# GLA state of 128 columns, output norms' Newton steps on GpSimd, and three smaller moves in a decoder trunk

## The chip, the cores and the metric

The kernel runs on one core of a Trainium2 chip, as one program and one launch. The metric is the device time in microseconds. Before the change the median of three runs is 2576.46 us (2575.63 to 2578.42). A core has TensorE (PE, with its weight loads shown as PEld), VectorE (DVE), ScalarE (ACT) and GpSimd (POOL); transfers are issued by SP, a few by POOL.

## The reference

One layer of a decoder trunk on x of 2048 x 1024 in float32, conditioned by a vector c:

- mod = silu(c) @ w_ada + b_ada gives six vectors of 1024: shift, scale and gate for each of two sub-layers.
- Token mixer: h = rmsnorm(x) (1 + sc1) + sh1; one input projection; then three groups of causal heads. Four retention heads (rotary q and k, fixed decay per head), eight HGRN2 heads (forget f = lb + (1 - lb) sigmoid(z), key (1 - f), 64 key channels), four GLA heads (decay exp(logsigmoid(...)/16), 32 key channels). All values have 64 columns per head. HGRN2 and GLA are the same recurrence with a decay per key channel:

```
S_t = diag(f_t) S_{t-1} + k_t^T v_t,   o_t = q_t S_t
```

- Each head's output is RMS-normed and multiplied by silu of a gate; the heads are joined, scaled by head_gain, and go through w_out; x += g1 * result.
- Channel mixer: norm and modulation again, up-projection to 2 x 2816, causal depthwise convolution of width 3, silu(gate) * value, down-projection; x += g2 * result. A final RMS norm with gain.

## The kernel before, in words

The sequence goes in four blocks of 512 positions (b = 0 to 3), each of four chunks of 128. Activations lie transposed (channels on the 128 partitions, positions along the columns). Every large product is made of three matmuls of a high and a low part (`split3`, L246 to L248). The token mixers take the first 1250 us; then the up and down products follow for two halves of the sequence.

A block runs the units h0, g, h1, h2, h3, r0, r1: two HGRN2 heads (h), all four GLA heads (g), two retention heads (r). A unit first makes its projections and query, key and decay tiles, then gives a chain of small steps (`gated`, `retention`) to a clock. The clock holds the order of TensorE, which is fixed by the program: it counts estimated microseconds of matmul time, and when a due time has passed, the next step of a chain is issued between the large matmuls. A step that comes too early on TensorE waits for the other engines. `LEVEL_GAP`, `POST_GAP` (12.0) and the `gap` of `rstd` are such due times. VectorE, ScalarE, GpSimd and SP are ordered by the planner of the framework, by priority and its own estimates (`tc.high_priority` moves instructions ahead); each runs its list in order.

`gated` works through seven levels (1, 2, 4 ... 64 positions): per level a matmul of keys with queries (L622), an update of the queries and keys by the decays (L630, L632), and a copy into the attention tile (L638, L641). Then the keys are transposed, the state gets its four updates (L671), `attn_out` adds attention times values and queries times state (L575 to L581), and `post` norms the output per head: square (L546), sum (L548), a reciprocal square root by a magic number and three Newton steps (`newton`, L153 to L158, each step three VectorE instructions), scaling (L552) and gate (L553). `transposed` (L559 to L562) brings it to channels on partitions, as high and low parts, for the output projection in two halves of four key tiles (`out_half`; the second half of block b comes after the first unit of block b + 1).

Query tiles `q` (128 x 2 x 512, a ring of three) hold head 0 in slot 0 and head 1 in slot 1, with zeros in the other head's rows, so that one matmul serves both heads. For HGRN2 both heads are merged into one tile `qn` before `attn_out` (L655), and the state has 128 columns, one block of 64 per head. For GLA the state has 64 columns, and each head has a matmul of its own with it (L581). GLA is done in two halves of two heads.

`ada` makes one of the 48 columns of mod: a load of 512 KB, a sum on VectorE (L197). The list `later` gives one to each weight piece that follows. Weights' low parts, and for w_out the high parts too, are made in block 0 and kept in HBM. `rstd` is the norm of a whole row: sums by a matmul (L325), Newton on VectorE, and after `gap` a broadcast by matmul (L335). `weight_sums` prepares sums of the channel mixer's weights. `vec` holds all per-channel vectors (245 columns).

Of the kernel before, what the change touches and what calls it, by code (L numbers as in the profile page):

```python
# [100 lines left out]
def trunk(ctx, tc, xT, vecs, cvec, cst, rope, msk, wada, win, walow, wgla, wout, wup, wdown, out):  # L101
# [38 lines left out]
    vec = pc.tile([P, NV], F32, tag="vec", name="vec")  # L140
    nc.sync.dma_start(vec[:], vecs)
    c_all = pc.tile([P, NC_], F32, tag="cst", name="c_all")
    m_all = p1.tile([P, 448], U32, tag="msk", name="m_all")
# [7 lines left out]
    def newton(x, y, n):  # L151

        V.tensor_scalar(y[:].bitcast(I32), x[:].bitcast(I32), -0.5, MAGIC, op0=ALU.mult, op1=ALU.add)  # L153
        a = small("nw", n)
        for _ in range(3):
            V.scalar_tensor_tensor(a[:], y[:], -0.5, y[:], op0=ALU.mult, op1=ALU.mult)
            V.tensor_tensor(a[:], a[:], x[:], op=ALU.mult)
            V.scalar_tensor_tensor(y[:], a[:], 1.5, y[:], op0=ALU.add, op1=ALU.mult)  # L158
# [53 lines left out]
    def piece(src, name, key, gain=None, ahead=50):  # L212

        if later:
            ada(later.pop(0))
        with tc.high_priority(offset=ahead):
            hi = pw.tile([P, 1024], F32R, tag="whi", name="h" + name)
            lo = pw.tile([P, 1024], F32R, tag="wlo", name="l" + name)
            if key + "h" in kept:
                nc.sync.dma_start(hi[:].bitcast(F32), kept[key + "h"][:])  # L220
                nc.sync.dma_start(lo[:].bitcast(F32), kept[key + "l"][:])
                return hi, lo
            raw = pw.tile([P, 1024], F32, tag="wraw", name="r" + name, bufs=NRAW)
            nc.sync.dma_start(raw[:], src)
            if gain is None:
                S.copy(hi[:], raw[:])
                if key + "l" in kept:
                    nc.sync.dma_start(lo[:].bitcast(F32), kept[key + "l"][:])
                else:
                    V.tensor_tensor(lo[:], raw[:], hi[:], op=ALU.subtract)  # L230
                    keep(key + "l", lo[:])
            else:
                n = 1024 // len(gain)
                for i, g in enumerate(gain):
                    sl = slice(i * n, (i + 1) * n)
                    S.activation(hi[:, sl], raw[:, sl], AF.Copy, scale=g)
                for i, g in enumerate(gain):
                    sl = slice(i * n, (i + 1) * n)
                    V.scalar_tensor_tensor(lo[:, sl], raw[:, sl], g, hi[:, sl], op0=ALU.mult, op1=ALU.subtract)
                keep(key + "h", hi[:])  # L240
                keep(key + "l", lo[:])
        return hi, lo
# [271 lines left out]
    states = [p1.tile([P, NS, 64 if i == 4 else P], F32, tag=f"S{i}", name=f"S{i}") for i in range(7)]  # L514
    for i, st in enumerate(states):
        if i != 4:
            G.memset(st[:], 0.0)
# [24 lines left out]
    def post(o, sg, name):  # L542
# [5 lines left out]
        V.tensor_reduce(ms[:], sq[:].rearrange("p (a e) -> p a e", e=64), axis=mybir.AxisListType.X, op=ALU.add)  # L548
        V.tensor_scalar(ms[:], ms[:], 1.0 / 64, EPS, op0=ALU.mult, op1=ALU.add)
        rs = small("ors" + name)  # L550
        newton(ms, rs, 8)
        V.tensor_tensor(o8, o8, rs[:].unsqueeze(2).to_broadcast([P, 8, 64]), op=ALU.mult)  # L552
        V.tensor_tensor(o[:], o[:], sg[:], op=ALU.mult)  # L553

    def transposed(b, pos, o, name):

        ps = late_ps("oT" + name)
        for c in range(NCH):
            T.transpose(ps[:, c * P:(c + 1) * P], o[:, c, :], ident)  # L559
        oT = pa.tile([P, 2, TB], F32R, tag="a4k", name="oT" + name)  # L560
        S.copy(oT[:, 0, :], ps[:])
        V.tensor_tensor(oT[:, 1, :], ps[:], oT[:, 0, :], op=ALU.subtract)  # L562
        oTs[b][pos] = oT

    def attn_out(name, b, attn, v, q, Sst, qn=None):

        ps = late_ps("o" + name)
        for c in range(NCH):
            oc = ps[:, c * P:(c + 1) * P]
            cs = slice(c * P, (c + 1) * P)  # L570
            inter = not (b == 0 and c == 0)
            both = inter and qn is not None
            st = Sst[:, (b * NCH + c) % NS, :]
            if both:
                T.matmul(oc, qn[:, cs], st, start=True, stop=False)  # L575
            for hh in range(2):
                oo = oc[:, hh * 64:hh * 64 + 64]
                T.matmul(oo, attn[:, (c * 2 + hh) * P:(c * 2 + hh + 1) * P], v[:, c, hh * 64:hh * 64 + 64],
                         start=not both, stop=hh == 1 if both else not inter)
                if inter and not both:  # L580
                    T.matmul(oo, q[:, hh, cs], st, start=False, stop=True)  # L581
        return ps
# [15 lines left out]
    def gated(name, b, ui, pos, kq, decay, subs, qk, sel):  # L598
# [45 lines left out]
        qn = None  # L644
# [4 lines left out]
        with tc.high_priority(offset=CHAIN):  # L649
            S.copy(kT[:].rearrange("p c n -> p (c n)"), ps[:])  # L650
            if not two:
                q, rows = subs[0][:2]
                qn = late("qn" + name)
                for hh, (r0, r1) in enumerate(rows):
                        S.copy(qn[r0:r1, :], q[r0:r1, hh, :])  # L655
        adv(4 * MF)
        yield 1.8
        for q, rows, v, sg in subs:
# [3 lines left out]
            with tc.high_priority(offset=CHAIN):  # L662
                for c in range(NCH):
                    for hh, (r0, r1) in enumerate(rows):
                        es = slice(0, 64) if two else slice(64 * hh, 64 * hh + 64)
# [10 lines left out]
        for i, ((q, rows, v, sg), at) in enumerate(zip(subs, attns)):  # L676
# [8 lines left out]
            ps = attn_out(f"{name}_{i}", b, at, v, q, Sst, qn)  # L685
# [13 lines left out]
    def unit_h(b, u, pos):  # L699
# [17 lines left out]
        q = new_qbd(nm, rows)  # L717
        for hh, (r0, r1) in enumerate(rows):
            V.tensor_tensor(q[r0:r1, hh, :], sq[r0:r1, :], f[r0:r1, :], op=ALU.mult)
# [16 lines left out]
    def unit_g(b, pos):  # L736
# [27 lines left out]
        V.tensor_tensor(qk[:], qs[:], kq[:], op=ALU.mult)  # L764
        decay = decays(f, e)
        subs = []
        for i in range(2):
            rows = [(32 * i, 32 * i + 32), (64 + 32 * i, 96 + 32 * i)]
            q = new_qbd(f"{nm}_{i}", rows)
            for hh, (r0, r1) in enumerate(rows):  # L770
                V.tensor_tensor(q[r0:r1, hh, :], qs[r0:r1, :], f[r0:r1, :], op=ALU.mult)
# [40 lines left out]
    def retention(nm, b, r, pos, a, kk, kc, q, vsg):  # L812
# [47 lines left out]
        ps = attn_out(nm, b, at, v, q, Sst, qn)  # L860
        o = pu.tile([P, NCH, P], F32, tag="o", name="o" + nm)
        qd = c_all[:, C_QD + 2 * r:C_QD + 2 * r + 2]
        with tc.high_priority(offset=CHAIN):
# [3 lines left out]
            post(o, sg, nm)  # L867
# [34 lines left out]
    def out_half(b, half, acc=None, after_pieces=None):  # L902
        hg = [vec[:, V_HG + 4 * half + k:V_HG + 4 * half + k + 1] for k in range(4)]
        ops = [oTs[b][4 * half + k] for k in range(4)]
        for i in range(4):
            wp = piece(wout[half * 4 + i], f"wo{b}_{half}_{i}", f"o{half * 4 + i}", gain=hg, ahead=250 if (b, half) == (0, 0) else 600 if (b, half) == (NB - 1, 1) else 50)
# [19 lines left out]
    def out_finish(b, after_pieces=None):  # L926
# [16 lines left out]
        clock.at(4.0, rstd(acc, f"n2_{b}", bc[:], then if b else lambda: put_off.append(then)))  # L943
# [90 lines left out]
    nc.sync.dma_start(m_all[:], msk)  # L1034
# [4 lines left out]
    for b in range(NB):  # L1039
        pos = 0  # L1040
        if b == 1:
            later += range(24, 40)
        if b == 2:
            later += range(40, 48)
        for i, (kind, u) in enumerate(ORDER):
# [6 lines left out]
            if b == 1 and i == 2:  # L1052
# [8 lines left out]
            if b and i >= (3 if b == 1 else 1):  # L1061
                for _ in range(2 if b == 2 else 1):
# [111 lines left out]
    def conv(s, u, t, y):  # L1174
        cw = vec[:, V_CW + 3 * t:V_CW + 3 * t + 3]
        S.activation(y[:], u[:, 2:SB + 2], AF.Identity, bias=vec[:, V_CB + t:V_CB + t + 1], scale=cw[:, 2:3])
# [98 lines left out]
    def down_norm(s, h, y, acc, bc, bank=None):  # L1275
        b = 2 * s + h

        def scale(m):
            V.scalar_tensor_tensor(y[h, m], y[h, m], vec[:, V_FG + m:V_FG + m + 1], bc[:], op0=ALU.mult, op1=ALU.mult)
# [25 lines left out]
    def last_product(s, y, acc):  # L1305
# [28 lines left out]
        def norm(t, p, sq, banks):  # L1334
# [11 lines left out]
            def scale(m, bc):  # L1346
                V.scalar_tensor_tensor(y[1, m][:, cols], y[1, m][:, cols], vec[:, V_FG + m:V_FG + m + 1], bc[:, 0:n],
# [82 lines left out]
    halo = pg.tile([P, 2 * NF + 4, 2], F32, tag="halo", name="halo")  # L1430
    with tc.high_priority(offset=100):
# [122 lines left out]
```

## Time and profile before

| | |
|---|---|
| median of three runs | 2576.46 us |
| profiled execution | 2570.92 us |
| its span in the trace | 2569.2 us |
| PE busy | 2500.8 us (97%) |
| DVE busy | 1990.3 us (77%) |
| ACT busy | 1117.5 us (43%) |
| POOL busy | 157.4 us (6%) |

The profile is one execution, taken by the hardware profiler. A row of a group gives line, engine, operation, tiles (out <- in), shapes and count, then busy us, mean ns of one, and the idle time before them with what ended it. A row of waits reads: engine, line, what it waited for, us in total, times, longest. A row of the timeline gives start, duration, engine, line, operation and tiles. A row on one source line gives min/median/max ns, first and last start. The time of the execution outside the span is 1.7 us.

### The profile page before, as it was taken

What the parts mean: (1) busy time and instruction counts of PE and PEld (TensorE: products, weight loads), DVE (VectorE), ACT (ScalarE), POOL (GpSimd) and SP (SyncE); (2) the same over time, 40 slices, a digit from 0 to 9 for tenths busy, and PEclk for the clock granted to TensorE, in tenths of its full rate; (3) what the DMA queues carried; (4) which work ended last, traced back from release to release, by engine and by line L of the source; (5) the groups of instructions that cost most, each with busy time, mean ns of one, the idle gap of its engine ahead of it and who ended that gap; (6) DMA issues with size and microseconds to landing.
All of it is one profiled execution on the core that took longest, in us unless ns stands there. A gap on an engine that the chain in (4) does not pass through costs nothing.

```text
span 2569.2 us, 37237 instructions
## 1 busy us (share of the span) xinstructions
PE 2500.8 (97%) x13206; PEld 2138.0 (83%) x13206; DVE 1990.3 (77%) x3648; ACT 1117.5 (43%) x1898; POOL 157.4 (6%) x270
## 2 busy tenths in 40 slices
PE   5999999999999999999999999999999999999998
PEld 4798878998889888998778888888878888888887
DVE  8778986868778786887678888887687778778666
ACT  3333434433343234433355545555444555455442
POOL 1000010000000000000010000000011001000000
PEclk9999999999999999999999999999999999999999
DMA  8543656765687856877664444477675444447653
GB/s 304 193 161 132 215 216 231 275 218 178 213 313 262 294 175 209 314 269 257 210 241 166 162 135 164 156 255 249 216 230 172 149 153 145 147 141 247 224 192 128
DMA packets 231242, 533.89 MB, mean 208 GB/s; under 512 B 25072, under 2 KB 28176, under 8 KB 231056
## 3 DMA queue, kind: packets, MB, share of 16 engines
q1 hardware_dynamic: 229136, 525.23, 60.0%
q0 software_dynamic: 1920, 6.29, 0.6%
q8 instruction: 104, 1.70, 0.3%
q14 instruction: 82, 0.67, 0.1%
HBM read 397.72 MB, written 133.69 MB: 207 GB/s over the span
## 4 chain that ended last, share of the span: by engine, by line
PE 87%; DVE 7%; DMA 3%; ACT 1%; issue 1%; SPq 0%; DVEq 0%; ACTq 0%
PE X L246 6%; PE X L247 6%; PE X L248 6%; PE lvh L622 3%; PE Z L247 3%; PE Z L246 3%; PE Z L248 3%; PE dX L247 3%; PE dX L246 3%; PE dX L248 3%; PE psqkvgr L248 2%; PE psqkvgr L246 2%; PE psqkvgr L247 2%; PE psvgh L246 2%; PE psvgh L247 2%; PE psvgh L248 2%
## 5 line engine op out<-in xcount | busy, mean ns | idle before, releaser
L246 PE MATMUL X<-B,A 128*128 128x512 f32 x572 | 223.9, 391 | 1.4 <-ACT u L1242 1.4
L247 PE MATMUL X<-B,A 128*128 128x512 f32 x572 | 223.2, 390 | 0.3 <-DMA B<-made 0.3
L248 PE MATMUL X<-B,A 128*128 128x512 f32 x572 | 223.1, 390 | 0.0
L973 DVE TENSOR_TENSOR dA<-rd,dA 128x512 fp32r<-128x512 f32 x154 | 106.0, 689 | 89.5 <-ACT dA L972 89.1
L972 ACT CAST dA<-rd 128x512 fp32r<-128x512 f32 x154 | 95.6, 621 | 142.8 <-PE dX L248 46.7
L973 DVE TENSOR_TENSOR A<-s,A 128x512 fp32r<-128x512 f32 x176 | 120.6, 686 | 40.7 <-ACT A L972 40.7
L246 PE MATMUL psvgh<-hvgh,ha 128*128 128x256 f32 x480 | 140.4, 293 | 0.0
L246 PE MATMUL dX<-dB,dA 128*128 128x512 f32 x352 | 136.9, 389 | 0.0
L247 PE MATMUL dX<-dB,dA 128*128 128x512 f32 x352 | 136.9, 389 | 0.0
L248 PE MATMUL dX<-dB,dA 128*128 128x512 f32 x352 | 136.9, 389 | 0.0
L248 PE MATMUL psvgh<-hvgh,ha 128*128 128x256 f32 x480 | 136.0, 283 | 0.0
L247 PE MATMUL psvgh<-lvgh,ha 128*128 128x256 f32 x480 | 136.0, 283 | 0.0
L972 ACT CAST A<-s 128x512 fp32r<-128x512 f32 x176 | 108.4, 617 | 62.6 <-PE Z L248 46.8
L246 PEld LDWEIGHTS X<-B,A 128*128 128x128 f32 x572 | 107.7, 188 | 25.3 <-ACT u L1242 2.2
L247 PEld LDWEIGHTS X<-B,A 128*128 128x128 f32 x572 | 107.7, 188 | 23.1 <-DMA B<-made 1.0
L248 PEld LDWEIGHTS X<-B,A 128*128 128x128 f32 x572 | 107.7, 188 | 22.3
L246 PE MATMUL Z<-B,A 128*128 128x512 f32 x308 | 120.6, 392 | 2.5 <-ACT B L972 1.7
L622 PEld LDWEIGHTS lvh<-qbh,kh 128*128 128x128 f32 x896 | 115.8, 191 | 7.5 <-issue 1.1
L247 PE MATMUL Z<-B,A 128*128 128x512 f32 x308 | 120.7, 392 | 0.3 <-DVE B L973 0.3
L622 PE MATMUL lvh<-qbh,kh 128*128 128x128 f32 x896 | 120.7, 277 | 0.3 <-DVE kh L632 0.3
L248 PE MATMUL Z<-B,A 128*128 128x512 f32 x308 | 120.4, 391 | 0.0
L973 DVE TENSOR_TENSOR dB<-rb,dB 128x512 fp32r<-128x512 f32 x154 | 105.3, 685 | 9.5 <-ACT dB L972 9.4
(457 smaller groups left out, 7133.3 us busy)
## 6 DMA issues: line engine op xcount, KB each, us to landing
gs<-yv SPq DMA_DIRECT2D x154, 256.0 KB, 2.9
rb<-gs SPq DMA_DIRECT2D x154, 256.0 KB, 4.0
r<-wup SPq DMA_DIRECT2D x141, 256.0 KB, 3.4
s<-sumsu SPq DMA_DIRECT2D x132, 256.0 KB, 3.0
wada<-wada SPq DMA_DIRECT2D x48, 512.0 KB, 4.8
rd<-sumsd SPq DMA_DIRECT2D x88, 256.0 KB, 4.0
rd<-wdown SPq DMA_DIRECT2D x66, 256.0 KB, 3.7
x<-xT SPq DMA_DIRECT2D x64, 256.0 KB, 4.8
```

Source lines behind the costliest of these rows:

```text
L246: T.matmul(ps, lhs[0], rhs[0], start=first, stop=False, skip_group_check=more)
L247: T.matmul(ps, lhs[0], rhs[1], start=False, stop=False, skip_group_check=more)
L248: T.matmul(ps, lhs[1], rhs[0], start=False, stop=last, skip_group_check=more)
L622: T.matmul(ps[:, c * P:(c + 1) * P].rearrange("p (h n s) -> p h n s", h=2, s=s), kq[:, c * P:(c + 1) * P], rhs, start=True, stop=True)
L972: S.copy(hi, src)
L973: V.tensor_tensor(lo, src, hi, op=ALU.subtract)
```

## The change

- The state of the GLA has 128 columns, like the others. The queries of the second head are copied into slot 0 at the end of the levels, for HGRN2 and GLA (the tile `qn` of HGRN2 is gone), and `attn_out` has one form: one matmul with the state per chunk, then one with the attention per head.
- `newton` has a form on GpSimd, with four instructions a step; `post` uses it, but for the last unit of the last block.
- Queries are multiplied by the decay once for all rows on VectorE; ScalarE then copies the heads into `q`.
- head_gain is applied where the outputs are transposed, no longer to the weights.
- The conditioning sums 24 to 39 begin after the first unit of block 1. The norm of block 0's rows that needs them moves from the third to the fourth unit of block 1, and weight sums begin one unit later, with two in the last unit.
- The norms of the blocks' inputs and of the rows of blocks 0 to 2 have a gap of 8.0 instead of 4.5 between their two steps on TensorE.
- `vec` holds 117 columns; convolution weights and final gain come in a second tile, loaded before the last output half. The mask tile loads 320 of 448 columns.

```diff
     def newton(x, y, n, relaxed=False):
         V.tensor_scalar(y[:].bitcast(I32), x[:].bitcast(I32), -0.5, MAGIC, op0=ALU.mult, op1=ALU.add)
         a = small("nw", n)
         for _ in range(3):
+            if relaxed:
+                G.tensor_tensor(a[:], y[:], y[:], op=ALU.mult)
+                G.tensor_tensor(a[:], a[:], x[:], op=ALU.mult)
+                G.tensor_scalar(a[:], a[:], -0.5, 1.5, op0=ALU.mult, op1=ALU.add)
+                G.tensor_tensor(y[:], a[:], y[:], op=ALU.mult)
+                continue
             V.scalar_tensor_tensor(a[:], y[:], -0.5, y[:], op0=ALU.mult, op1=ALU.mult)
...
-        clock.at(22.0, rstd(acc, f"n1_{b}", bc1[b][:], lambda: done.add(("n1", b))))
+        clock.at(22.0, rstd(acc, f"n1_{b}", bc1[b][:], lambda: done.add(("n1", b)), gap=8.0))
...
-    states = [p1.tile([P, NS, 64 if i == 4 else P], F32, tag=f"S{i}", name=f"S{i}") for i in range(7)]
+    states = [p1.tile([P, NS, P], F32, tag=f"S{i}", name=f"S{i}") for i in range(7)]
...
-        newton(ms, rs, 8)
+        newton(ms, rs, 8, relaxed)
...
-        S.copy(oT[:, 0, :], ps[:])
-        V.tensor_tensor(oT[:, 1, :], ps[:], oT[:, 0, :], op=ALU.subtract)
+        g = vec[:, V_HG + pos:V_HG + pos + 1]
+        S.activation(oT[:, 0, :], ps[:], AF.Copy, scale=g)
+        V.scalar_tensor_tensor(oT[:, 1, :], ps[:], g, oT[:, 0, :], op0=ALU.mult, op1=ALU.subtract)
...
-    def attn_out(name, b, attn, v, q, Sst, qn=None):
+    def attn_out(name, b, attn, v, qn, Sst):
         ps = late_ps("o" + name)
         for c in range(NCH):
             oc = ps[:, c * P:(c + 1) * P]
             inter = not (b == 0 and c == 0)
-            both = inter and qn is not None
-            if both:
-                T.matmul(oc, qn[:, cs], st, start=True, stop=False)
+            if inter:
+                T.matmul(oc, qn[:, c * P:(c + 1) * P], Sst[:, (b * NCH + c) % NS, :], start=True, stop=False)
             for hh in range(2):
...
-                if inter and not both:
-                    T.matmul(oo, q[:, hh, cs], st, start=False, stop=True)
...
-            if not two:
-                q, rows = subs[0][:2]
-                qn = late("qn" + name)
-                for hh, (r0, r1) in enumerate(rows):
-                        S.copy(qn[r0:r1, :], q[r0:r1, hh, :])
+            for q, rows, v, sg in subs:
+                r0, r1 = rows[1]
+                S.copy(q[r0:r1, 0, :], q[r0:r1, 1, :])
...
+        V.tensor_tensor(sq[:], sq[:], f[:], op=ALU.mult)
         for hh, (r0, r1) in enumerate(rows):
-            V.tensor_tensor(q[r0:r1, hh, :], sq[r0:r1, :], f[r0:r1, :], op=ALU.mult)
+            S.copy(q[r0:r1, hh, :], sq[r0:r1, :])
...
-            post(o, sg, nm)
+            post(o, sg, nm, (b, r) != (NB - 1, 1))
...
-            wp = piece(wout[half * 4 + i], f"wo{b}_{half}_{i}", f"o{half * 4 + i}", gain=hg, ahead=...)
+            wp = piece(wout[half * 4 + i], f"wo{b}_{half}_{i}", f"o{half * 4 + i}", both=True, ahead=...)
...
-        clock.at(4.0, rstd(acc, f"n2_{b}", bc[:], then if b else lambda: put_off.append(then)))
+        clock.at(4.0, rstd(acc, f"n2_{b}", bc[:], then if b else lambda: put_off.append(then), gap=8.0 if b < NB - 1 else 4.5))
...
-        if b == 1:
-            later += range(24, 40)
...
+            if b == 1 and i == 0:
+                later += range(24, 40)
-            if b == 1 and i == 2:
+            if b == 1 and i == 3:
                 assert not later
                 clock.until(lambda: put_off)
                 put_off.pop()()
...
-            if b and i >= (3 if b == 1 else 1):
-                for _ in range(2 if b == 2 else 1):
+            if b and i >= (4 if b == 1 else 1):
+                for _ in range(2 if b == 2 or (b, i) == (1, 6) else 1):
                     weight_sums(*jobs.pop(0))
...
+    vec2 = pg.tile([P, NV - V_CW], F32, tag="vec2", name="vec2")
+    nc.sync.dma_start(vec2[:], vecs[:, V_CW:NV])
```

GLA's query part has the same form as HGRN2's, with two halves of 32 rows per head.

More of the change, by code (lines that the diff above doesn't have):

```diff
@@ L210, in trunk, with piece @@
     later = []
-    def piece(src, name, key, gain=None, ahead=50):
+    def piece(src, name, key, both=False, ahead=50):
         if later:
@@ L224, in piece @@
             nc.sync.dma_start(raw[:], src)
[L225 to L231, printed above, removed]
-            else:
[L233 to L240, printed above, removed]
+            S.copy(hi[:], raw[:])
+            if key + "l" in kept:
+                nc.sync.dma_start(lo[:].bitcast(F32), kept[key + "l"][:])
+            else:
+                V.tensor_tensor(lo[:], raw[:], hi[:], op=ALU.subtract)
+                if both:
+                    keep(key + "h", hi[:])
                 keep(key + "l", lo[:])
@@ L540, in tok_evac4, with post @@
             V.tensor_tensor(sg[:, c, :], sg[:, c, :], gate, op=ALU.mult)
-    def post(o, sg, name):
+    def post(o, sg, name, relaxed=True):
         o8 = o[:].rearrange("p c (h e) -> p (c h) e", e=64)
@@ L770, in unit_g @@
             for hh, (r0, r1) in enumerate(rows):
[L771 removed]
+                S.copy(q[r0:r1, hh, :], qs[r0:r1, :])
             subs.append((q, rows, *tok_tiles(f"{nm}_{i}")))
@@ L902, in out_half @@
     def out_half(b, half, acc=None, after_pieces=None):
-        hg = [vec[:, V_HG + 4 * half + k:V_HG + 4 * half + k + 1] for k in range(4)]
         ops = [oTs[b][4 * half + k] for k in range(4)]
         for i in range(4):
-            wp = piece(wout[half * 4 + i], f"wo{b}_{half}_{i}", f"o{half * 4 + i}", gain=hg, ahead=250 if (b, half) == (0, 0) else 600 if (b, half) == (NB - 1, 1) else 50)
+            wp = piece(wout[half * 4 + i], f"wo{b}_{half}_{i}", f"o{half * 4 + i}", both=True, ahead=250 if (b, half) == (0, 0) else 600 if (b, half) == (NB - 1, 1) else 50)
             if i == 3 and after_pieces:
@@ L1174, in conv @@
     def conv(s, u, t, y):
-        cw = vec[:, V_CW + 3 * t:V_CW + 3 * t + 3]
-        S.activation(y[:], u[:, 2:SB + 2], AF.Identity, bias=vec[:, V_CB + t:V_CB + t + 1], scale=cw[:, 2:3])
+        cw = vec2[:, 3 * t:3 * t + 3]
+        S.activation(y[:], u[:, 2:SB + 2], AF.Identity, bias=vec2[:, V_CB - V_CW + t:V_CB - V_CW + t + 1], scale=cw[:, 2:3])
         V.scalar_tensor_tensor(y[:], u[:, 1:SB + 1], cw[:, 1:2], y[:], op0=ALU.mult, op1=ALU.add)
```

34 lines of the change are left out of this document (15 added, 19 removed).

## The prediction

> **What bounds the kernel now.** I read the page's span and busy times first, then a table of three stretches, then TensorE's own waits in the middle one, where the change acts.
>
> ```profile
> span 2569.2 us, 37237 instructions
> ...
> PE 2500.8 (97%) x13206; PEld 2138.0 (83%) x13206; DVE 1990.3 (77%) x3648; ACT 1117.5 (43%) x1898; POOL 157.4 (6%) x270
> ...
> PE 87%; DVE 7%; DMA 3%; ACT 1%; issue 1%; SPq 0%; DVEq 0%; ACTq 0%
> ```
>
> ```profile
> 0.00:64.00 64.00, 37.26 (x179) 29.90 (x180) 52.39 (x92) 23.19 (x35) 11.44 (x23) 0.97 0.83 304
> 64.00:1250.00 1186.00, 1168.40 (x7252) 1036.24 (x7251) 924.14 (x2130) 448.08 (x856) 56.04 (x94) 1.00 0.65 227
> ```
>
> ```profile
> PE pshfh L246 <- ACT sgg L539: 3.0, 1, 3.0
> PE oTh L559 <- DVE oh L553: 2.7, 2, 2.5
> PE pshfh L246 <- ACT ha L356: 2.6, 1, 2.6
> ...
> PE pshfh L247 <- DVE ha L359: 1.6, 1, 1.6
> ...
> PE bcn L335 <- DVE rsn L158: 1.2, 2, 0.9
> PE oTr L559 <- DVE or L553: 0.8, 1, 0.8
> PE oTr L559 <- DVE or L864: 0.8, 1, 0.8
> PE lvh L622 <- DVE kh L632: 0.3, 1, 0.3
> ```
>
> The second fence gives, for a stretch, the busy us of PE, PEld, DVE, ACT and POOL, then clock, DMA share and GB/s. From 64 to 1250 us (the token mixers) TensorE is busy for 1168.4 of 1186 us, so it is the bound; VectorE has 924 us (78%), ScalarE 448 and GpSimd 56. Time saved on VectorE or ScalarE counts only where TensorE stood waiting for it, and in this stretch that is under 18 us. What counts at once is a matmul less.
>
> The change moves work in five ways. I price each on the path of TensorE.
>
> **A. GLA state of 128 columns: matmuls less.** Before, each chunk and GLA half had two inter-chunk matmuls of 64 columns (L581) and two of attention (L578). After, one inter matmul of 128 columns serves both heads, the form that HGRN2 already has (L575). A 32-bit matmul shows as two records, "x2".
>
> ```profile
> L581 PE MATMUL og<-S,qbg x120: 275/275/275, 175.7 to 1099.1; 128*128 128x64 f32 x120
> ```
>
> ```profile
> 479.14 0.39 PE L581 MATMUL og<-S,qbg 128*128 128x64 f32 x2
> 479.37 0.39 PE L578 MATMUL og<-vg,atg 128*128 128x64 f32 x2
> 479.59 0.39 PE L581 MATMUL og<-S,qbg 128*128 128x64 f32 x2
> ```
>
> ```profile
> 529.15 0.44 PE L575 MATMUL oh<-S,qnh 128*128 128x128 f32 x2
> 529.43 0.56 PE L578 MATMUL oh<-vh,ath 128*128 128x64 f32 x4
> 529.82 0.44 PE L575 MATMUL oh<-S,qnh 128*128 128x128 f32 x2
> ```
>
> Start to start a 64-column matmul of the GLA takes 0.225 us (479.14 to 479.59 holds two). The HGRN2 chunk, one of 128 and two of 64 columns, takes 0.67 us (529.15 to 529.82), so the 128-column one takes 0.67 - 2 x 0.225 = 0.22 us: the same. 120 records are 60 matmuls; they become 30. Saved: 30 x 0.22 = **6.7 us**, on the bounding engine. The Trainium skill, "TensorE: Matmul & The Clock Gate", section "Back-to-back issue gap", says the gap goes with the columns, about 60 cycles for up to 64 and 134 for 128. By it two halves cost what one whole costs and A saves nothing. The rows disagree, and I go by the rows.
>
> **B. The start of block 1.** The waits "pshfh <- ha" (2.6 and 1.6 us) are one place, near 326 us. VectorE there:
>
> ```profile
> 322.02 0.16 DVE L549 TENSOR_SCALAR omsr<-omsr 128x8 f32<-128x8 f32 x1
> ...
> 325.17 0.17 DVE L158 SCALAR_TENSOR_TENSOR orsr<-nw,orsr 128x8 f32<-128x8 f32 x1
> 325.26 0.74 DVE L352 SCALAR_TENSOR_TENSOR xn<-xn,mod,bc 128x512 f32<-128x512 f32 x1
> ...
> 326.79 1.28 DVE L197 CUSTOM_DVE_ANT_0 wada<-wada,c_act,vec 128x1024 f32<-128x1024 f32 x1
> ...
> 328.07 0.74 DVE L359 SCALAR_TENSOR_TENSOR ha<-xn,mod,ha 128x512 fp32r<-128x512 f32 x1
> ```
>
> The last input scaling (L352) waits behind a Newton iteration interleaved with state updates, and the last low part (L359) behind a conditioning sum of 1.28 us. The change takes the Newton steps to GpSimd and starts the 16 conditioning sums of block 1 after its first unit, four pieces later. Both covers of this wait go. I take 3.0 of the 4.2 us; bounds 0 and 4.2. The moved sums (16 x 1.28 us and their 512 KB loads on SP's queue) now reach into the third and fourth units of block 1. With them move the block-0 norm's eight output rows, with their stores, and one weight-sum job. VectorE gains more there than it takes on, so 0; the bound is one late level per unit, 2 us lost.
>
> **C. Broadcast of the norms.** The wait "bcn <- rsn" (1.2 us, two times) goes when the second step of that norm comes 8.0 instead of 4.5 us after the first; TensorE runs other matmuls of its list in between. Its consumers follow tens of us later in the order of issue. I take -1.2; bounds -1.2 and 0.
>
> **D. Newton on GpSimd: the doubtful part.** 31 of 32 output norms lose nine VectorE steps and gain twelve GpSimd steps; seed and final scaling (L552, L553) stay on VectorE, and the transposes (L559) follow. A tight post:
>
> ```profile
> 881.41 0.68 DVE L548 TENSOR_REDUCE omsh<-osqh 128x8 f32<-128x512 f32 x1
> ...
> 883.77 0.16 DVE L153 TENSOR_SCALAR orsh<-omsh 128x8 int32<-128x8 int32 x1
> ...
> 889.36 0.69 DVE L552 TENSOR_TENSOR oh<-oh,orsh 128x512 f32<-128x512 f32 x1
> ...
> 890.57 0.68 DVE L553 TENSOR_TENSOR oh<-oh,sgh 128x512 f32<-128x512 f32 x1
> ```
>
> ```profile
> 891.40 0.63 PE L559 MATMUL oTh<-c_all,oh 128*128 128x128 f32 x4 [0.23 <-DVE oh L553]
> ...
> 892.56 1.05 PE L622 MATMUL lvh<-qbh,kh 128*128 128x128 f32 x8
> ```
>
> From the end of the seed (883.93) to L552 pass 5.4 us now, though the nine steps are short: VectorE does other work between them.
>
> ```profile
> L156 DVE SCALAR_TENSOR_TENSOR nw<-orsh 128x8 f32<-128x8 f32 x48 | 8.0, 167 | 0.6
> ```
>
> ```profile
> L1224 POOL COPY uv<-halo x22: 186/186/418, 1912.6 to 2318.8; 128x2 f32<-128x2 f32 x22
> L1224 POOL COPY ug<-halo x22: 1084/1688/1842, 1913.7 to 2331.2; 128x2 f32<-128x2 f32 x22
> ```
>
> ```profile
> L1180 POOL COPY halo<-ug x22: 572/578/3512, 1289.0 to 1696.5; 128x2 f32<-128x2 f32 x22
> ```
>
> No GpSimd arithmetic is in this trace. The nearest rows are these copies of two columns: 0.19 us beside a quiet VectorE, 0.58 in the median when it begins behind a 512-column VectorE instruction, 1.69 behind longer ones, 3.5 at worst. So twelve steps take 2.2 us (L552 3.2 us earlier than now), 6.9 us (1.5 later) or 20 us (15 later). The Trainium skill, "SBUF — State Buffer", section "Who interferes with whom", says that a GpSimd read and a VectorE instruction with two SBUF inputs hold one port as a lock, the later one standing still until the other ends. The copies agree, and by that rule alone the 6.9 us is the one to take.
>
> I take a mixture, because VectorE runs its list in order: if it comes to L552 too early it stands still, and GpSimd then goes at 0.19. Half and half: 6 x 0.58 + 6 x 0.19 = 4.6 us, L552 0.8 us earlier than now, VectorE parked for about 1.1 us. Behind it in its queue are the next unit's level updates (L630, L632); TensorE's level matmul waits for those. In the post shown that level has its last update end at 891.59 and its matmul start at 892.56, room of 1.0 us, so a parked 1.1 us costs 0.1 there. I charge 0.2 us for each of the 31: 6.2 us; the old waits of L559 that a shorter chain removes (2.7 + 0.8 of the rows above) give back 3.5. Sum **+2.7**. Bounds: -3.5, and +25 when L552 comes 3 us late on average, by the rival below. GpSimd's memsets for the next units' queries stand in the same queue, but they wait for a matmul that comes ahead of the post, as now.
>
> **E. Queries times decay once.** HGRN2: one VectorE product over 128 partitions and two ScalarE copies, instead of two products; GLA: one product and four copies, instead of four products. At the end of the levels ScalarE merges the heads with one copy instead of two (HGRN2), two instead of none (GLA).
>
> ```profile
> 650.42 1.38 DVE L719 TENSOR_TENSOR qbh<-sqh,fh 64x512 f32<-64x512 f32 x2
> ```
>
> ```profile
> 653.60 1.16 PE L622 MATMUL lvh<-qbh,kh 128*128 128x128 f32 x8
> ```
>
> ```profile
> L655 ACT COPY qnh<-qbh 64x512 f32<-64x512 f32 x32 | 19.8, 617 | 5.4 <-DVE qbh L630 4.5 <-DVE nw L156 0.6
> ```
>
> In this unit the queries end at 651.80 and the first level starts at 653.60: 1.8 us of room. The new way is one product (0.69) and two copies (2 x 0.62) where two products took 1.38, so 0.5 us later, and it fits: 0 on the path. If ScalarE's queue holds it up by more than the rest, a unit loses that; bound 2 us.
>
> **F. The rest.** The heads' scale goes from the output weights (made once, in block 0) to the transposed outputs, inside instructions that exist already; none of TensorE's waits names either. The vector table comes in two loads; the second stands in SP's queue before the last output half: +0.3 of 0 to 2 us, since a "made" operand behind it is already 0.5 and 0.3 us late there.
>
> ```profile
> PE X L247 <- DMA lB<-made: 0.5, 1, 0.5
> PE X L247 <- DMA B<-made: 0.3, 2, 0.2
> ```
>
> **Sum**: -6.7 - 3.0 - 1.2 + 2.7 + 0 + 0.3 = -7.9 us. The profiled execution took 2570.92 us (span 2569.2 and 1.7 around it), so 2563.0 for such a one; the median of the runs, 2576.46, is 5.5 us above it, and with the same saving gives **2568.6 us**.
>
> **Rivals.**
> - *More of the waits go* (0.19): VectorE loses 31 x 9 steps of 0.167 us (47 us), GpSimd keeps near 0.19 us a step. D is then -3.5 instead of +2.7: 2562. For it: the waits are few and of VectorE's making. Against it: the 0.58.
> - *The gain is eaten at L552* (0.19): GpSimd's twelve steps are held, VectorE parks up to 12 x 0.19 = 2.3 us, the room of 1.0 covers less than half, and of the 1.3 left a third, 0.4 us a post, reaches TensorE, without L559's old waits going: D = 12.4, total +1.8, 2578. For it: the row with 3.5 us. Against it: VectorE has 22% of idle time to catch up.
> - *Slower: L559 becomes late everywhere* (0.13). Place: the transposes after each post. Each step takes 0.7 us, since GpSimd is let in only between VectorE's instructions, and L552 comes 3 us later than now. Posts like the one shown lose 2.8 us each, those with more than 3 us of room nothing; I take 0.8 between these ends, over 31 posts 25 us, total -10.6 + 25 = +14, 2591. It decides from about 0.6 us a step (7.3 us, 1.9 late). For it: the 0.58. Against it: parking frees the port.
> - *Widening saves nothing* (0.04): a 128-column matmul takes 0.45 us, twice the 64-column one, so the 30 merged ones cost what the 60 did. -7.9 + 6.7 = -1.2, 2575. Against it: the HGRN2 chunk's 0.67 us. The Trainium skill's rule under A comes to the same.
>
> **Chances and range.** The forecast has 0.45. A change under 0.2% (5.2 us) can't be told from none here: faster means below 2571.3 us. The forecast gives 0.38 of its 0.45 to faster and 0.07 to the same; the first rival's 0.19 are all faster; the second gives 0.14 to the same and 0.05 to slower; the third is slower (0.13); the last is the same (0.04). In sum 0.57, 0.25 and 0.18. The range takes in the first two rivals and most of the unknown bounds, leaving out the slow tail and A to D all at their best: 2557 to 2584. The forecast's own range is 2563 to 2574.
>
> **What would show it.** A: GLA inter matmuls x60 records of 128 columns, and a chunk of 0.67 us. B: no wait on "ha" at the start of block 1. C: no "bcn" wait before 1250 us. D: the mean of a GpSimd step (0.2, 0.4, 0.6 or more), VectorE's idle time before L552 put down to GpSimd, and the waits of L559 and L622. E: no wait of L622 on a ScalarE copy. The prediction is wrong if L559 or L622 wait for more than 15 us in sum, or if the 128-column matmuls take longer than 0.22 us.

## The result and the profile after

The changed kernel takes **2599.98 us** in the median (2595.76 to 2604.18), the kernel before 2576.46: a ratio of **1.0091, 95% interval 1.0079 to 1.0102**. It is 23.5 us slower, where the prediction had 2568.6 us and a range up to 2584. The profiled execution took 2595.76 us.

The page of the changed kernel, with its span, its busy times and the chain that ended last:

```profile
span 2594.0 us, 37194 instructions
...
PE 2504.1 (97%) x13146; PEld 2135.3 (82%) x13146; DVE 1944.6 (75%) x3317; ACT 1140.0 (44%) x1914; POOL 249.8 (10%) x643
...
PE 78%; DVE 10%; DMA 5%; POOL 3%; issue 3%; ACT 2%; SPq 0%; DVEq 0%; POOLq 0%; ACTq 0%
```

The work went where the diff says. TensorE has 60 records less (13206 to 13146), VectorE 331 instructions less and 46 us less busy time, GpSimd 92 us more. And yet GpSimd now stands on the chain that ended last, with 3%, and VectorE has 10% of it instead of 7%.

TensorE's waits in the token mixers (64 to 1280 us) of the changed kernel: who waits, for whom, us in total, times, longest:

```profile
PE lvh L613 <- DVE kh L623: 22.5, 14, 4.1
PE pshfh L243 <- ACT sgg L535: 3.6, 1, 3.6
PE oTr L555 <- DVE or L549: 3.1, 1, 3.1
PE lvh L613 <- ACT qbh L708: 3.0, 2, 2.0
...
PE bcn L332 <- ACT doth L604: 0.5, 2, 0.3
PE oTh L555 <- DVE oh L549: 0.4, 1, 0.4
```

L613 and L623 are L622 and L632 of before: the level matmul of HGRN2 and the key product of the level ahead of it. That wait was 0.3 us, one time. The transposes (L555, before L559) wait for less than before: for HGRN2 0.4 us instead of 2.7, and the 3.1 us are those of the last unit, whose steps stay on VectorE (3.0 before). The waits on "ha" are gone. VectorE's own waits in the same stretch say why L623 is late:

```profile
DVE oh L548 <- POOL orsh L160: 33.2, 16, 3.5
...
DVE og L548 <- POOL orsg L160: 19.4, 8, 3.5
...
DVE or L548 <- POOL orsr L160: 14.2, 7, 2.6
```

L548 (before L552) scales an output by its norm. VectorE stands in front of it for 33.2 + 19.4 + 14.2 = **66.8 us**, at every one of the 31 norms whose Newton steps are on GpSimd: 2.15 us each. One such place on GpSimd, on VectorE and on TensorE:

```profile
183.23 1.85 POOL L157 TENSOR_TENSOR nw<-orsg 128x8 f32<-128x8 f32 x1 [4.27 <-DVE orsg L153]
185.16 0.20 POOL L158 TENSOR_TENSOR nw<-nw,omsg 128x8 f32<-128x8 f32 x1
185.45 0.20 POOL L159 TENSOR_SCALAR nw<-nw 128x8 f32<-128x8 f32 x1
...
187.98 0.20 POOL L160 TENSOR_TENSOR orsg<-nw,orsg 128x8 f32<-128x8 f32 x1
```

```profile
183.20 0.69 DVE L343 TENSOR_TENSOR san<-san,sqn 128x512 f32<-128x512 f32 x1
183.80 1.22 DVE L235 TENSOR_TENSOR lvgh<-rvgh,hvgh 128x1024 fp32r<-128x1024 f32 x1
188.21 0.69 DVE L548 TENSOR_TENSOR og<-og,orsg 128x512 f32<-128x512 f32 x1 [3.19 <-POOL orsg L160]
188.82 0.69 DVE L621 TENSOR_TENSOR qbh<-qbh,eh 128x512 f32<-128x512 f32 x1
189.42 0.68 DVE L549 TENSOR_TENSOR og<-og,sgg 128x512 f32<-128x512 f32 x1
190.03 0.42 DVE L623 TENSOR_TENSOR kh<-kh,eh 128x256 f32<-128x256 f32 x1
```

```profile
182.02 1.07 PE L613 MATMUL lvh<-qbh,kh 128*128 128x128 f32 x8
...
186.14 0.39 PE L245 MATMUL pshfh<-ha,lhfh 128*128 128x512 f32 x1
190.59 2.04 PE L613 MATMUL lvh<-qbh,kh 128*128 128x128 f32 x8 [4.06 <-DVE kh L623]
192.29 0.77 PE L243 MATMUL pshqh<-ha,hhqh 128*128 128x512 f32 x1
```

This is to be read from the bottom up. TensorE stops for 4.06 us, until the key product (L623) is done. It and the query product ahead of it (L621) could have begun at 185.0: the matmul of the level before ended at 183.1 (182.02 + 1.07) and VectorE's own last work at 185.02 (183.80 + 1.22). But they stand in VectorE's list behind L548, and there VectorE waits for 3.19 us, until GpSimd's last step. GpSimd's steps start 0.28 us apart (185.16, 185.45), so twelve of them take 3.3 us by themselves; the first took 1.85 us here, beside two VectorE instructions with two large operands (L343 and L235). Over the 31 norms GpSimd's last step ends 4.15 us after the seed in the mean, and VectorE has come to the scaling after 2.0. Between the seed (L153) and the scaling VectorE now has 4.3 other instructions on average in its order of issue (0 to 8). Before it had 9.1 (2 to 16) beside the nine Newton steps. So the list was made thinner where more time has to pass. (With two iterations or one on GpSimd, in two of the experiments, it is 3.2 and 2.2: the planner leaves less in between for a shorter chain, and on average too little each time.)

### The profile page after: what moved, and what is told of

Same layout as the page of the kernel before. It is cut to its first block, busy times and chain, and to the rows that moved or that the text cites. A ratio compares the mean times of both kernels' runs of the same rounds, so it can differ in the third digit from the quotient of the medians.

```text
span 2594.0 us, 37194 instructions
## 1 busy us (share of the span) xinstructions
PE 2504.1 (97%) x13146; PEld 2135.3 (82%) x13146; DVE 1944.6 (75%) x3317; ACT 1140.0 (44%) x1914; POOL 249.8 (10%) x643
## 4 chain that ended last, share of the span: by engine, by line
PE 78%; DVE 10%; DMA 5%; POOL 3%; issue 3%; ACT 2%; SPq 0%; DVEq 0%; POOLq 0%; ACTq 0%
PE X L243 6%; PE X L245 6%; PE X L244 6%; PE lvh L613 3%; PE Z L244 3%; PE Z L245 3%; PE Z L243 3%; PE dX L245 3%; PE dX L244 3%; PE dX L243 3%; PE lvg L613 2%; PE psvgh L243 2%; PE psvgh L244 2%; PE psvgh L245 2%; PE dY L245 2%
## 5 line engine op out<-in xcount | busy, mean ns | idle before, releaser
L613 PE MATMUL lvh<-qbh,kh 128*128 128x128 f32 x896 | 122.7, 280 | 25.6 <-DVE kh L623 22.5
L613 PEld LDWEIGHTS lvh<-qbh,kh 128*128 128x128 f32 x896 | 115.5, 192 | 37.4 <-issue 22.4
```

The lines of the kernel that those rows point to most:

```text
L613: T.matmul(ps[:, c * P:(c + 1) * P].rearrange("p (h n s) -> p h n s", h=2, s=s), kq[:, c * P:(c + 1) * P], rhs, start=True, stop=True)
```

## The experiments

Nine kernels. In the fences of this part the line numbers are those of the kernel named; the line of the norm's last GpSimd step is L160 in every kernel that waits for it.

**Newton steps on VectorE, all else as changed.**

```
-        newton(ms, rs, 8, relaxed)
+        newton(ms, rs, 8)
```

> The changed kernel with the Newton steps of all output norms back on VectorE, everything else kept. Theory P (VectorE stands still in front of the scaling of an output, waiting for GpSimd, and the level updates behind it come late): all of the loss goes and the other parts show their gain, 2562 to 2568 us, ratio to before 0.995 to 0.997, no wait of TensorE's level matmuls on the key update over 2 us in sum. Theory O (the other moves cost: copies of the queries on ScalarE, conditioning and norm moved within block 1): it stays above before, 2578 to 2600 us.

Measured: 2561.34 us (2560.2 to 2563.12), ratio to before 0.9944 [0.9929, 0.996]. One argument makes the changed kernel 38.6 us faster than it is, and faster than the kernel before, by a little more than expected. The mixers of this kernel and then of the changed one, up to the last transpose (the columns: stretch, its length, busy us and records of PE, PEld, DVE, ACT, POOL, then clock, DMA share, GB/s):

```profile
64.00:1245.10 1181.10, 1162.90 (x7200) 1029.94 (x7198) 912.74 (x2088) 469.74 (x871) 55.96 (x94) 1.00 0.65 229
```

```profile
64.00:1278.90 1214.90, 1172.94 (x7199) 1035.08 (x7197) 882.72 (x1809) 469.52 (x871) 148.15 (x466) 0.99 0.64 222
```

The mixers end 33.8 us later with the steps on GpSimd, and the two profiled spans differ by the same 33.8, so nothing of the loss lies outside. TensorE's idle time is 1214.90 - 1172.94 = 42.0 us instead of 18.2; its wait on L623 falls from 22.5 to this:

```profile
PE lvh L613 <- DVE kh L623: 1.7, 3, 0.7
```

That wait alone is thus 20.8 us of the 33.8. The other 10.0 us are busy time, for as many matmuls; the last section comes back to them.

**The Newton steps alone, in the kernel before** (31 of 32 norms; the diff is that of newton(), post() and its last call, and nothing else of the change).

> The kernel before with nothing but the Newton steps of 31 output norms on GpSimd. Theory P: VectorE is parked about 2 us in each of 31 norms as in the changed kernel (67 us in sum there), TensorE loses what the changed kernel lost plus the gains that the other parts gave it: 2605 to 2615 us, ratio 1.011 to 1.015. Theory O: near before, 2575 to 2585 us.

Measured: 2611.09 us, ratio 1.0141 [1.0127, 1.0155]. Alone the edit costs 36 us (33 to 40), as much as the first run gives back. With the first run's -14 us by its ratio the two make +22, against 23.5 measured, so the parts hardly act on each other. TensorE waits where it waits in the changed kernel, and a second wait grows:

```profile
PE lvh L628 <- DVE kh L638: 18.8, 15, 2.1
PE bcn L341 <- DVE rsn L164: 6.6, 5, 2.7
```

**No wait for the steps.** GpSimd does the twelve steps, on a tile of its own, and the scaling takes the seed.

```
-        for _ in range(3):
+        z = small("nz", n) if relaxed else None
+        for i in range(3):
             if relaxed:
-                G.tensor_tensor(a[:], y[:], y[:], op=ALU.mult)
+                w = z if i else y
+                G.tensor_tensor(a[:], w[:], w[:], op=ALU.mult)
...
-                G.tensor_tensor(y[:], a[:], y[:], op=ALU.mult)
+                G.tensor_tensor(z[:], a[:], w[:], op=ALU.mult)
```

> The changed kernel, in which GpSimd does the same twelve steps on a tile of its own and VectorE scales the output with the seed of the iteration, so that it has nothing to wait for; the three Newton steps are left out of the result. Theory P: as with the steps back on VectorE or a little better, 2558 to 2568 us. Rival C (the GpSimd steps hold the port that VectorE's second input needs, and slow its instructions): the loss stays to a good part, over 2580 us, and the mean of VectorE's two-input instructions rises above 0.69 us.

Measured: 2561.72 us, ratio 0.9946 [0.9932, 0.9959], as fast as with the steps on VectorE. GpSimd executes as many instructions beside the same VectorE work, and nothing is lost. The mixers of this kernel, to be read beside the changed kernel's row above:

```profile
64.00:1244.20 1180.20, 1163.19 (x7198) 1030.59 (x7197) 883.60 (x1809) 470.10 (x871) 196.41 (x466) 1.00 0.66 229
```

VectorE needs 883.6 us for its 1809 instructions, where it needed 882.7. GpSimd needs 196.4 for its 466, where it needed 148.2: its steps take 0.38 us in the mean instead of 0.25 when VectorE doesn't stand still beside them. So the two engines do get in each other's way here, but it is GpSimd that loses by it, and that costs nothing when nothing waits for GpSimd. The loss of the changed kernel is the wait.

**The GLA state of 128 columns alone, in the kernel before** (with the two loads of the vector table and the smaller mask, which make the room for it, and the merging copies of ScalarE).

> The kernel before with the GLA state of 128 columns alone, and the vector table in two loads that makes room for it. The matmul rows say 30 matmuls of 0.22 us less: 2568 to 2572 us, ratio 0.9970 to 0.9985. If a 128-column matmul costs twice a 64-column one: 2575 to 2579 us, ratio 0.9995 to 1.001.

Measured: 2567.21 us, ratio 0.9968 [0.9956, 0.9981]: -8.2 us (-11 to -5). That is at the good end of what was expected (2568 to 2572 us). All 60 records have 128 columns, and one has the 275 ns in the median that the 64-column one had before:

```profile
L571 PE MATMUL og<-S,qbg x60: 272/275/348, 174.2 to 1092.6; 128*128 128x128 f32 x60
```

A GLA chunk takes 0.67 us from start to start in the median, here and in the changed kernel, as the HGRN2 chunk did.

**Scaling and gate on GpSimd too**, so that VectorE has nothing to wait for at this place.

```
-        V.tensor_tensor(o8, o8, rs[:].unsqueeze(2).to_broadcast([P, 8, 64]), op=ALU.mult)
-        V.tensor_tensor(o[:], o[:], sg[:], op=ALU.mult)
+        E = G if relaxed else V
+        E.tensor_tensor(o8, o8, rs[:].unsqueeze(2).to_broadcast([P, 8, 64]), op=ALU.mult)
+        E.tensor_tensor(o[:], o[:], sg[:], op=ALU.mult)
```

> The changed kernel with the scaling and the gate of those 31 outputs on GpSimd too, behind its own Newton steps, so that VectorE waits for none of it. Theory P: the level updates are on time again, TensorE's waits on the key update fall from 22.5 us to under 5; GpSimd's two instructions of 512 columns lengthen the way to the transposes, of which most have 3 us of room or more: 2558 to 2575 us. Rival C (GpSimd's reading slows VectorE): two instructions of 512 columns read far more than twelve of 8, and the time is over 2590 us.

Measured: 2576.95 us, ratio 1.0009 [0.9999, 1.002]. Some 60% of the loss is gone, and 16 us stay, which is more than expected (2558 to 2575 us). Groups of this kernel (busy us, mean ns):

```profile
L550 POOL TENSOR_TENSOR oh<-oh,sgh 128x512 f32<-128x512 f32 x16 | 24.3, 1519 | 1.3
L549 POOL TENSOR_TENSOR oh<-oh,orsh 128x512 f32<-128x512 f32 x16 | 17.2, 1072 | 1.3
```

```profile
PE lvh L614 <- DVE kh L624: 4.7, 6, 2.0
...
PE oTh L556 <- POOL oh L550: 3.5, 4, 1.3
```

The wait on the level update falls from 22.5 to 4.7 us, and a new one on the gate appears, since GpSimd takes 1.5 us for what VectorE does in 0.68. Here contention does reach VectorE: 15 of its products over 128x512 in the mixers take 0.9 to 1.8 us beside GpSimd's, instead of 0.69, and some of them are level updates:

```profile
490.07 1.72 POOL L550 TENSOR_TENSOR og<-og,sgg 128x512 f32<-128x512 f32 x1
490.54 1.80 DVE L622 TENSOR_TENSOR qbh<-qbh,eh 128x512 f32<-128x512 f32 x1
```

Together these 15 are 11 us longer. How much of the 16 us comes from that, and how much from the longer way to the transposes, wasn't separated.

**Scaling and gate put later in VectorE's list**: they are handed to the planner 8 us later by the clock's estimate, and issued behind the newest level update, mask, row sum or key instruction that is there by then (mark[0] holds it).

```
+                with tc.issue_after(mark[0].ins):
+                    scale()
...
+        def scale():
+            V.tensor_tensor(o8, o8, rs[:].unsqueeze(2).to_broadcast([P, 8, 64]), op=ALU.mult)
+            V.tensor_tensor(o[:], o[:], sg[:], op=ALU.mult)
...
+        yield 8.0
+        finish(ps_)
+        yield POST_GAP - 8.0
```

> The changed kernel, its Newton steps on GpSimd, but the scaling and the gate put later in VectorE's queue: traced 8 us of TensorE's estimated time after the norm and queued behind the newest level update, score mask, row addition or key instruction traced by then. Theory P: the idle time of VectorE in front of the scaling falls from 67 us in sum to under 25, and the time to 2558 to 2570 us. If parking is not the cause, nothing of the loss goes: 2590 to 2600 us.

Measured: 2565.14 us, ratio 0.9955 [0.9941, 0.9968]. The engines do the work of the changed kernel, and only the order of issue differs. VectorE's waits for GpSimd fall to a third:

```profile
DVE oh L564 <- POOL orsh L160: 12.1, 9, 2.6
...
DVE or L564 <- POOL orsr L160: 6.8, 3, 2.6
...
DVE og L564 <- POOL orsg L160: 3.5, 4, 0.9
```

**One Newton iteration instead of three on GpSimd** (four steps; range(3) becomes range(1 if relaxed else 3)).

> The changed kernel with one Newton step instead of three on GpSimd (four instructions instead of twelve; two steps are left out of the result). Theory P: four instructions at the 0.28 us that twelve took each are 1.1 us instead of 3.3; VectorE is parked for under 1 us a norm, 15 to 30 us in sum, which the room before the level matmuls covers for the most part: 2560 to 2572 us. If the handover between the engines is what costs, not the steps: over 2585 us.

Measured: 2563.47 us, ratio 0.9951 [0.9938, 0.9965].

```profile
DVE oh L548 <- POOL orsh L160: 9.1, 13, 0.9
...
DVE og L548 <- POOL orsg L160: 5.9, 6, 1.2
...
DVE or L548 <- POOL orsr L160: 3.6, 6, 1.2
```

Parked (standing in front of the scaling) for 18.6 us in sum, VectorE costs about 1 us against the kernel without the wait. At the rate of the changed kernel it would be 10. So parked time isn't lost at a fixed rate.

**Two iterations** (eight steps), to see from where it is lost.

> The changed kernel with two Newton iterations instead of three on GpSimd (the third is left out, so the norms are less exact): eight dependent small steps, about 2.2 us at the pitch of 0.28, instead of 3.3. It asks how parked VectorE time turns into run time. Known: no waiting 2561.7, one iteration 18.6 us parked over 31 posts and 2563.5, three iterations 66.8 us and 2600. Theory room: each post has about 1 us of room before the level updates become TensorE's bound, as the post shown in the prediction had, and all that is parked beyond it reaches the end. I expect about 40 us parked (1.3 a post), so 31 x 0.3 = 9 us lost: 2571 (2567 to 2575). Rival proportional from the first microsecond: 38 / 66.8 = 0.57 of what is parked, 23 us lost: 2584 (2579 to 2588). In between (2575 to 2579): the room differs from post to post, and neither holds alone.

Measured: 2579.21 us (ten runs), ratio 1.0013 [1.0, 1.0026]. Taken as it stood, this speaks against the theory of a room (2571, 2567 to 2575): it lies where the band for neither theory ends and that of the proportional rival (2579 to 2588) begins. But the time parked was more than expected, 22.0 + 13.9 + 9.8 = 45.7 us where 40 had been guessed:

```profile
DVE oh L548 <- POOL orsh L160: 22.0, 15, 2.4
...
DVE og L548 <- POOL orsg L160: 13.9, 8, 2.4
...
DVE or L548 <- POOL orsr L160: 9.8, 7, 2.4
```

With it the four kernels line up. The loss is the ratio less the 0.9946 of the kernel without the wait, times 2576 us; the column before it takes 1.0 us of room a post (one output norm), by the 31 posts, from what was parked:

| iterations on GpSimd | parked, us | a post, us | parked beyond 1.0 a post, us | measured loss, us |
|---|---|---|---|---|
| none waited for | 0 | 0 | 0 | 0 |
| one | 18.6 | 0.60 | 0 | 1 |
| two | 45.7 | 1.47 | 14.7 | 17 |
| three (the change) | 66.8 | 2.15 | 35.8 | 37 |

Each loss has about 5 us of uncertainty. A fixed share of what is parked (37 / 66.8) would give 10 and 25 in the middle rows, which the first of them excludes and the second is at the edge of. A room of 1.0 us a post, with all beyond it lost, fits all four. Counted post by post instead of by the mean, 0.5, 16.7 and 36.3 us lie beyond the room. Since the guess of 40 us was part of the expectation, this agreement is found afterwards and not foretold. Two kernels that it wasn't made from bear on it. With the Newton steps alone in the kernel before, 65.6 us are parked, 35.3 of them beyond 1.0 a post, and 36 (33 to 40) are lost. With the later scaling 8.1 us lie beyond, and the loss is 2 (about 5 of uncertainty): there the level updates come first, and the room may well be larger. What is lost isn't one wait, either: TensorE's wait on L623 makes 2.8, 10.8 and 22.5 us in the kernels with one, two and three iterations (2.0 without the wait), and the rest is mostly longer busy time.

**The conditioning of block 1 back to its old place**, with the Newton steps on VectorE. The block-0 norm's rows and the weight sums go back with it.

```
+        if b == 1:
+            later += range(24, 40)
...
-            if b == 1 and i == 0:
-                later += range(24, 40)
-            if b == 1 and i == 3:
+            if b == 1 and i == 2:
```

> The changed kernel with the Newton steps on VectorE and also the conditioning sums, the block-0 norm and the weight sums of block 1 back in their old places. If the later conditioning is worth what the prediction's part B says (3 us of 4.2), TensorE's waits on the inputs at the start of block 1 are back (2.6 and 1.6 us) and the time is 2 to 5 us above that of the kernel with the Newton steps on VectorE alone, 2563 to 2567 us; if it is worth nothing, 2560 to 2563 us.

Measured: 2570.85 us, ratio 0.9983 [0.9974, 0.9992], so 9.5 us slower than the first kernel of this list, and above both ranges that were expected. But the waits on "ha" (2.6 and 1.6 us before) didn't come back. In their place stands one wait of another kind:

```profile
PE pshqh L243 <- ACT hhqh L231: 7.2, 1, 7.2
```

The loads on SP's queue of this kernel show what is late:

```profile
318.95 0.33 SPq L233 DMA_DIRECT2D lvgh<-kepti3l  x1
320.84 0.33 SPq L230 DMA_DIRECT2D rhqh<-win  x1
```

The weights of the next product (rhqh) stand behind a load (kepti3l) that waits until 318.95 for its buffer. In the kernel before, the weights rhqh went out at 300.81. So this run shows that the start of block 1 is worth up to 10 us by the order of loads, and not what the conditioning by itself is worth.

## Why the prediction was wrong

**D failed, and it alone decides the sign.** It stood at +2.7 us with a bound of +25; alone it measures +36 (33 to 40), and inside the change 2599.98 - 2561.34 = 38.6. The sign of being wrong that the prediction named came too: L622 (now L613) waits for 22.5 us on the key product, more than 15. Its mechanism was named: VectorE runs its list in order, parks at L552 (now L548), and the level updates behind it come late. The failure is in two of its sizes.

- *How long VectorE parks.* I took 1.1 us a post, from a chain of 4.6 us against an L552 that comes 5.4 us after the seed. The recorded working doesn't show how the 1.1 comes out of these two: the nine steps of 0.167 us off the 5.4 leave 3.9, which gives 0.7. Either way VectorE was taken to be there 3.5 us or more after the seed. The chain was not longer than that estimate: 4.15 us in the mean. VectorE came earlier, after 2.0. I subtracted the nine steps from its list and left the scaling's place among the others as it was, though the order of issue is planned anew: 9.1 other instructions in between became 4.3. Parked were 2.15 us.
- *What of it reaches TensorE.* The room of 1.0 us read from the one post shown was right as a mean. But I charged 0.2 us a post on top of a parked 1.1, and the second rival a third of the 1.3 beyond the room. By the table as much is lost as lies beyond: 2.15 - 1.0 = 1.15 us, by 31 posts 36 us. The rival "the gain is eaten at L552" thus had the right place and nearly the right parked time (up to 2.3 us), and would have come out at 2606 without its "a third" (31 x 1.3 = 40 instead of 12.4). My reason against the full price, VectorE's 22% of idle time, doesn't help: at 185.0 us the level's two products could have begun, and they stood behind L548 for the 3.19 us that VectorE was idle.

The 3.5 us that D gives back, the old waits of L559, did come for the most part: 2.7 became 0.4, and the 0.8 on L553 is gone.

**A was right.** Predicted -6.7 us, measured -8.2 (-11 to -5) together with the second table load. The sixty records of 128 columns have the median 275 ns that those of 64 columns had, so the rival "widening saves nothing" is refuted.

**B** was right about its two waits: both "ha" rows are in the GLA-alone kernel still, and in none with the new place. With the Newton steps alone on GpSimd one of them stays, with 3.3 us, so the steps' move doesn't remove them by itself. How much of that is the later conditioning and how much the order of the loads wasn't separated.

**C** holds: no "bcn" wait on VectorE is left in the changed kernel, and where the Newton steps moved without the longer gap it grew from 1.2 us to 6.6.

**E** shows no such wait with the Newton steps on VectorE, nor where nothing waits for GpSimd. In the changed kernel the level matmul does wait for a ScalarE copy of the queries (L708, 3.0 us in two waits), against "no wait". With two iterations it is 1.8 us and with the later scaling 2.6; with one iteration it isn't there. So E probably used up room that the parked VectorE then lacked; its own price wasn't measured alone.

A, B, C, E and F together were to give -10.6 us and gave -14 (-18 to -10). F wasn't measured alone.

**The third rival**, transposes late everywhere, had the right sign and the wrong place. The transposes kept their slack (0.4 and 3.1 us of waits, the latter at the last unit); the instructions queued behind the scaling did not. Steps held at 0.7 us, its condition, didn't occur: by the groups of the changed kernel a step takes 0.20 to 0.37 us in the mean. What it had against itself, that parking frees GpSimd, is borne out: 0.25 us a step where VectorE parks, 0.38 where it doesn't.

```profile
L159 POOL TENSOR_SCALAR nw<-nw 128x8 f32<-128x8 f32 x93 | 21.4, 230 | 8.1
...
L157 POOL TENSOR_TENSOR nw<-orsg 128x8 f32<-128x8 f32 x24 | 8.9, 370 | 23.2 <-DVE orsg L153 16.2 <-DVE eh L586 5.9
```

The best kernel of the study is the change with its Newton steps left on VectorE: 2561.34 us.

## What to carry to other kernels

Moving a dependent chain of small instructions to an idle engine takes busy time from the first engine, but it puts a wait for the whole chain into that engine's list, and everything behind the wait stops with it. Price such a move by the time from the chain's start to the instruction that needs it, in the new order of issue, and compare it with the slack of what is queued behind that instruction; in this kernel what exceeded the slack was lost about in full, at every occurrence. If the chain has to move, move the consumer back in the list as well, as the run with the later scaling did.

## What the runs showed of the hardware beside that

**A stop of TensorE can cost more than its length.** Here are the stretches around the wait of 4.06 us in the changed kernel (the clock is the third number from the end):

```profile
186.00:190.60 4.60, 0.54 (x4) 0.15 (x2) 2.39 (x5) 1.54 (x2) 2.49 (x9) 0.88 0.62 216
190.60:193.00 2.40, 2.40 (x10) 2.30 (x11) 2.40 (x3) 0.77 (x2) 0.00 (x0) 0.50 0.00 0
193.00:196.00 3.00, 3.00 (x9) 2.32 (x8) 1.86 (x4) 0.46 (x1) 0.00 (x0) 0.50 0.62 203
196.00:200.00 4.00, 4.00 (x25) 3.35 (x24) 3.06 (x6) 1.32 (x2) 0.00 (x0) 0.96 0.31 114
```

After the stop the granted clock is 0.50 for 5.4 us, which loses 2.7 us on top of the wait. A stop of 3.0 us in the kernel before (pshfh <- sgg, in the prediction's rows) is followed by a clock of 1.00:

```profile
739.10:742.00 2.90, 2.61 (x12) 2.21 (x13) 2.63 (x7) 0.56 (x4) 0.00 (x0) 1.00 0.96 328
```

But length alone doesn't decide it. In the kernel with two iterations a stop of 2.53 us, up to 489.0, is followed by a clock of 0.50, and one of 3.51 us, up to 1047.0, by 1.00:

```profile
489.00:492.00 3.00, 2.96 (x14) 2.96 (x15) 2.13 (x3) 0.00 (x0) 2.35 (x9) 0.50 0.93 239
```

```profile
1047.00:1050.00 3.00, 3.00 (x13) 2.49 (x14) 2.86 (x7) 0.28 (x2) 0.00 (x0) 1.00 0.82 332
```

The Trainium skill, "TensorE: Matmul & The Clock Gate", section "Why this matters for your kernels", advises against idle gaps of TensorE over about 3 us, since the clock then falls to half. The first two of these stops agree with it, the other two don't, so in this case about 3 us is no sharp bound. Over the whole span the mean clock is 0.992 in the changed kernel and 0.994 with the steps on VectorE, which is about 5 us (0.008 x 2594 less 0.006 x 2560), of some 33 us that the change's Newton steps cost there. In the mixers alone TensorE is busy at a clock of 0.50 for 19.9 us in the changed kernel and for 6.4 with the steps on VectorE. At half speed that is 6.8 us lost, about two thirds of the 10.0 us of longer busy time. The other third I can't place.

**Small GpSimd steps** of 128x8 show a duration of 0.20 us and start 0.28 us apart when they depend on each other and VectorE leaves them alone; the copies that I had taken for the nearest row gave 0.19. A GpSimd product over 128x512 took 1.07 us with the broadcast norm and 1.52 with the gate, where VectorE took 0.69 and 0.68.
